# A four-layer decoder trunk on one core: the weights' parts begin at eight places, 4 bytes apart, and rotate through ten slots instead of eleven

## The chip, the cores and the metric

The kernel runs on one core of one Trainium2 chip. The metric is device time in microseconds (us) of one execution; the lower the better. The time before is 1584.25 us, the median of two runs (1583.47 and 1585.03 us).

Engines: PE (TensorE, matrix products), PEld (its loads of the stationary operand, which overlap the products), ACT (ScalarE), DVE (VectorE), POOL (GpSimd), SP (issues transfers).

## What is computed

Four residual layers over 256 tokens of width 1024, everything in float32. The token mixer is attention in layers 0 and 3, a gated short convolution in layer 1, a Conformer convolution in layer 2. A gated feed-forward block (FFN) of width 2816 follows in every layer.

```
def conv_ffn(x, w_in, w_conv, w_out):
    u = causal_dwconv(x @ w_in, w_conv)
    g, v = jnp.split(u, 2, axis=-1)
    return (jax.nn.silu(g) * v) @ w_out

    for i in range(DEPTH):
        a = rms_norm(h, mix_norm_pre[i])
        m = mixer of layer i (a)
        h = h + rms_norm(m, mix_norm_post[i])
        f = conv_ffn(rms_norm(h, ffn_norm_pre[i]), ffn_w_in[i], ffn_w_conv[i], ffn_w_out[i])
        h = h + rms_norm(f, ffn_norm_post[i])
```

## The kernel before, in words

**Products.** Activations lie transposed, 128 features on the partitions and 256 tokens along them. A float32 product is made of three products in the type float32r: every operand is split into a coarse part `hi` and a remainder `lo`, and `mm3` (L280 to L282) adds `hi`·x`hi`, `hi`·x`lo` and `lo`·x`hi` in PSUM. A weight block of 128 x 128 is the stationary operand and 256 columns of activations stream past it. `ramp` (L433, L438, L440) does the same in another order at a stage's start, and `Slabs.mm` (L522) for the FFN's second matrix. In attention's values (L878 to L880) the roles are exchanged: activations are stationary and 256 columns of weights stream. Each of these products loads its stationary operand anew.

**The stream of weights.** `Stream` hands the weights out in 480 pieces of 128 x 1024 float32, each used by 24 products. A piece is half of a 1 MB block `raw` (three buffers) that SP fetches from HBM. `first` (L186 to L194) lets ACT copy the piece to `whi` (L192, a cast), and `second` (L196 to L199) lets DVE form `wlo` = `raw` - `whi` (L198). Both parts go to rotating slots, `SLOTS` = 11 of each. `take` hands over the next piece and makes one on the spot if none is ready. `copy`, `diff` and `pump` are called between other work and make pieces in advance, as long as this holds:

```
if self.copied < min(len(self.pieces), self.used - self.held + self.slots - margin):
```

With `margin` = 1 at most 10 pieces are copied beyond those taken. No piece is made in `boundary`, the norm between two stages, except at the kernel's very start; what was made before must last until the next stage's calls of `between` (one `diff`, one `copy`).

**Order.** The whole program runs under a manual schedule: each engine executes its instructions in the order in which the code issues them. There is no planner.

**Addresses.** All tiles lie in fixed places. In the built program every `whi` and `wlo` slot begins 32 bytes past a multiple of 128 bytes on its partition, and every activation tile 96 bytes past one. A pad named `gap` (112 float32) at the head of the activations' pool fixes that distance of 64.

Of the kernel before, what the change touches and what calls it, by code (L numbers as in the profile page):

```python
# [11 lines left out]
F32R = mybir.dt.float32r  # L12
# [4 lines left out]
P = 128  # L17
# [3 lines left out]
KD = D // P  # L21
# [9 lines left out]
EPS_LN = 1e-5  # L31
BIG = 1e30
HKF = KF // 2
SLOTS = 11
NACT = 32
PE_TAPS = (13, 13, 13, 15)
SPLIT = 60
FIRST = 10
# [29 lines left out]
def plan():  # L68

    nt = 3 * NH * DH  # L70
    for l in range(DEPTH):
        kind, j = l % 3, l // 3
        if kind == 0:
            for quad in range(NQ):
                for what, g in order(quad):
                    if what == "v":
                        for k0 in (0, 4):
                            yield "attn_w_qkv", j, k0, 4, 2 * nt + (g * NH + 4 * quad) * DH, 2 * P
                    else:
                        c = (g * NH + 4 * quad + 2 * (what == "b")) * DH  # L80
                        yield "attn_w_qkv", j, 0, KD, c, P
                        yield "attn_w_qkv", j, 0, KD, nt + c, P
            for d in range(KD):
                yield "attn_w_o", j, 0, KD, d * P, P
        elif kind == 1:
            for step in sc_steps():
                if step[0] == "col":
                    for c in (D, 2 * D, 0):
                        yield "sc_w_in", j, 0, KD, c + step[1] * P, P
                elif step[0] == "slab":  # L90
                    yield "sc_w_out", j, step[1], 1, 0, D
                elif step[1] % 2 == 0:
                    yield "sc_w_out", j, SC_HEAD, KD - SC_HEAD, step[1] * P, 2 * P
        else:
            for k in range(KD):
                yield "cc_w_pw1", j, 0, KD, k * P, P
                yield "cc_w_pw1", j, 0, KD, D + k * P, P
            for d in range(KD):
                yield "cc_w_pw2", j, 0, KD, d * P, P
        for step in ffn_steps():  # L100
            if step[0] == "col":
                for c in (0, F):
                    yield "ffn_w_in", l, 0, KD, c + step[1] * P, P
            elif step[0] == "slab":
                yield "ffn_w_out", l, step[1], 1, 0, D
            else:
                yield "ffn_w_out", l, FF_HEAD, KF - FF_HEAD, step[1] * P, P
# [37 lines left out]
class Stream:  # L145
# [40 lines left out]
    def first(self):  # L186
        b, c, n = self.pieces[self.copied]
        self.load(b + self.ahead)
        hi = self.w_pool.tile([P, KD * P], F32R, tag="whi", name="whi")[:, :n * P]
        lo = self.w_pool.tile([P, KD * P], F32R, tag="wlo", name="wlo")[:, :n * P]  # L190
        raw = self.raw[b][:, c:c + n * P]
        self.nc.scalar.copy(out=hi, in_=raw)  # L192
        self.parts[self.copied] = hi, lo, raw
        self.copied += 1  # L194

    def second(self):  # L196
        hi, lo, raw = self.parts[self.prepped]
        self.nc.vector.tensor_tensor(out=lo, in0=raw, in1=hi.bitcast(F32), op=ALU.subtract)  # L198
        self.prepped += 1  # L199

    def copy(self, margin=1):
        if self.copied < min(len(self.pieces), self.used - self.held + self.slots - margin):
            self.first()
# [25 lines left out]
def trunk_kernel(ctx: ExitStack, tc: tile.TileContext, xT, pos, params, consts, masks, w8, out):  # L229
    nc = tc.nc  # L230
    cp = ctx.enter_context(tc.tile_pool(name="cp", bufs=1))
    rawp = ctx.enter_context(tc.tile_pool(name="rawp", bufs=3))
    wp = ctx.enter_context(tc.tile_pool(name="wp", bufs=SLOTS))
    ap = ctx.enter_context(tc.tile_pool(name="ap", bufs=1))
    ps = ctx.enter_context(tc.tile_pool(name="ps", bufs=1, space=bass.MemoryType.PSUM))
    ap.tile([P, 112], F32, tag="gap", name="gap")

    st = Stream(nc, rawp, wp, SLOTS, 3, [w8[i] for i in range(w8.shape[0])])
    for _, _, _, nk, _, cols in plan():
# [20 lines left out]

    def act(dt=F32, tag="act", bufs=NACT, shape=(P, 2, T)):
        counter[0] += 1
        return ap.tile(list(shape), dt, tag=tag, name=f"{tag}{counter[0]}", bufs=bufs)
# [15 lines left out]
    def mm3(o, whi, wlo, x, first, last):  # L279
        nc.tensor.matmul(o, lhsT=whi, rhs=x[0], start=first, stop=False)  # L280
        nc.tensor.matmul(o, lhsT=whi, rhs=x[1], start=False, stop=False)  # L281
        nc.tensor.matmul(o, lhsT=wlo, rhs=x[0], start=False, stop=last)  # L282
# [142 lines left out]
    def ramp(xs, os, hook=None):  # L425


        ws = [st.take() for _ in os]
        alone = [i == 0 or os[i - 1].tensor is not o.tensor for i, o in enumerate(os)]

        def second(k):
            for o, (whi, wlo, _) in zip(os, ws):
                nc.tensor.matmul(o, lhsT=whi[:, k, :], rhs=xs[k][1], start=False, stop=k == KD - 1,  # L433
                                 skip_group_check=True)

        for k in range(KD):
            for o, (whi, wlo, _), a in zip(os, ws, alone):
                nc.tensor.matmul(o, lhsT=whi[:, k, :], rhs=xs[k][0], start=k == 0 and a, stop=False,  # L438
                                 skip_group_check=True)
                nc.tensor.matmul(o, lhsT=wlo[:, k, :], rhs=xs[k][0], start=False, stop=False,  # L440
                                 skip_group_check=True)
            if k:
                second(k - 1)
        if hook:
            hook()
        second(KD - 1)
        return os
# [212 lines left out]
    def conformer(l, mg, rb):  # L660
# [7 lines left out]
        def cols(q, hook=None):  # L668
            if q > 1:
                banks[q % 2] = [psum("A") for _ in range(2)]  # L670
            for bank in banks[q % 2]:
                for o in halves(bank):
                    column(xs, o, hook)
                    hook = None
# [50 lines left out]

        mine = [list(range(CONV - 1 - n, CONV - 1)) for n in PE_TAPS]
        rest = [list(range(CONV - 1 - n)) for n in PE_TAPS]
        cols(1, scale)
# [65 lines left out]
    def attention(l, mg, rb):  # L794
# [125 lines left out]
        def weigh(pair, pts):  # L920
            o = psum("B")
            quad, q2 = divmod(pair, 2)

            def mm(hp, g, kc, cols, blk, first, last):
                col = (2 * q2 + hp) * DH
                nc.tensor.matmul(o[hp * DH:(hp + 1) * DH, cols], lhsT=vs[quad, g][:, kc, col:col + DH],  # L926
                                 rhs=pts[hp][blk // 2][:, blk % 2, cols], start=first, stop=last)

            for kc in range(2):
                for hp in range(2):  # L930
                    mm(hp, 0, kc, slice(0, T), kc, kc == 0, False)
            for g in (1, 2):
                for c in range(2):
                    for hp in range(2):
                        mm(hp, g, c, slice(c * P, (c + 1) * P), 1 + g, False, g == 2 and c == 1)
            ys[pair] = two()
            split(ys[pair], o[:, :T])
# [264 lines left out]
```

## Time and profile before

| | before |
|---|---|
| median of two runs | 1584.25 us |
| the profiled execution: its own time | 1583.57 us |
| the profiled execution: span, first to last instruction | 1581.7 us |
| PE busy | 1555.7 us (98%) |
| DVE busy | 1243.0 us (79%) |
| ACT busy | 925.2 us (58%) |
| read from HBM | 253.87 MB |

The span is what the rows below add up to; some 1.9 us of the execution lie around it. Products overlap in the profile: one lasts some 280 ns, but the next begins after 113 to 118 ns, so the pace is read from starts, not from durations. In the rows, `psA` and `psB` are PSUM tiles, `act` and `tmp` are activations, `raw`, `whi` and `wlo` are the stream's tiles.

### The profile page before, as it was taken

The page shows a single profiled execution, that of the slowest core. Times are in us where ns is not written, and L with a number is a line of the kernel's source. Part 1 is how long each engine was busy: PE and PEld are TensorE (multiplying, and loading weights), DVE is VectorE, ACT ScalarE, POOL GpSimd, SP SyncE. Part 2 cuts the span into 40 slices and gives each one's busy share as a digit, 9 for nine tenths or more (in the row PEclk, how much of TensorE's full clock was granted, in tenths as well). Part 3 has the DMA queues.
Part 4 walks back from the last instruction along what each step waited for, and adds up shares of the span by engine and source line. Part 5 has one row for each costly group of instructions (what it writes and reads, how often), then busy time and mean ns, then how long its engine had stood idle before and what let it go on. Part 6 is the DMA issues. An engine that isn't in the chain of part 4 may idle for free.

```text
span 1581.7 us, 31426 instructions
## 1 busy us (share of the span) xinstructions
PE 1555.7 (98%) x13146; PEld 1520.5 (96%) x13146; DVE 1243.0 (79%) x2177; ACT 925.2 (58%) x1623; POOL 17.9 (1%) x51
## 2 busy tenths in 40 slices
PE   6999999999999999999999999999999999999998
PEld 6999999999999999999999999999999999999997
DVE  4997877697876779889599598786887778588783
ACT  6564655575564566656477666565655445566562
POOL 4000000000000000000000000000000000000000
PEclk9999999999999999999999999999999999999999
DMA  5653543265552644655243136554453434236540
GB/s 218 216 212 131 176 145 108 99 232 204 187 190 100 217 161 162 238 187 184 110 144 124 54 118 239 197 174 153 178 192 138 161 134 160 107 134 237 190 160 28
DMA packets 36718, 256.94 MB, mean 162 GB/s; under 512 B 4320, under 2 KB 4448, under 8 KB 5984
## 3 DMA queue, kind: packets, MB, share of 16 engines
q1 hardware_dynamic: 36288, 254.93, 45.0%
q8 instruction: 103, 1.69, 0.4%
q14 instruction: 39, 0.32, 0.1%
q10 hardware_dynamic: 288, 0.01, 0.0%
HBM read 253.87 MB, written 1.05 MB: 161 GB/s over the span
## 4 chain that ended last, share of the span: by engine, by line
PE 93%; DVE 3%; ACT 1%; POOL 1%; issue 1%; DMA 1%; DVEq 0%; ACTq 0%; POOLq 0%
PE psA L522 17%; PE psB L282 10%; PE psB L280 10%; PE psB L281 10%; PE psA L280 7%; PE psA L281 7%; PE psA L282 7%; PE psA L878 3%; PE psA L880 3%; PE psA L879 3%; PE psB L715 2%; PE psB L926 2%; PE psB L897 2%; PE psA L438 2%; PE psB L915 2%; PE psA L433 2%
## 5 line engine op out<-in xcount | busy, mean ns | idle before, releaser
L198 DVE TENSOR_TENSOR wlo<-raw,whi 128x1024 fp32r<-128x1024 f32 x480 | 580.7, 1221 | 35.3 <-ACT whi L192 34.4
L192 ACT CAST whi<-raw 128x1024 fp32r<-128x1024 f32 x480 | 490.9, 1048 | 23.8 <-DMA raw<-in_w_dram 18.7
L282 PE MATMUL psB<-act,wlo 128*128 128x256 f32 x1392 | 390.7, 281 | 0.0
L280 PE MATMUL psB<-act,whi 128*128 128x256 f32 x1392 | 390.7, 281 | 0.0
L281 PE MATMUL psB<-act,whi 128*128 128x256 f32 x1392 | 390.7, 281 | 0.0
L280 PE MATMUL psA<-act,whi 128*128 128x256 f32 x1040 | 299.2, 288 | 8.0 <-ACT whi L192 7.1
L282 PE MATMUL psA<-act,wlo 128*128 128x256 f32 x1040 | 290.7, 280 | 0.5 <-DVE wlo L198 0.5
L281 PE MATMUL psA<-act,whi 128*128 128x256 f32 x1040 | 290.8, 280 | 0.2
L522 PE MATMUL psA<-act,whi 128*128 128x256 f32 x1536 | 272.9, 281 | 0.0
L281 PEld LDWEIGHTS psB<-act,whi 128*128 128x128 f32 x1392 | 265.0, 190 | 0.0
L282 PEld LDWEIGHTS psB<-act,wlo 128*128 128x128 f32 x1392 | 263.1, 189 | 0.0
L280 PEld LDWEIGHTS psB<-act,whi 128*128 128x128 f32 x1392 | 261.3, 188 | 0.0
L522 PEld LDWEIGHTS psA<-act,whi 128*128 128x128 f32 x1536 | 236.2, 189 | 0.0
L522 PE MATMUL psA<-act,wlo 128*128 128x256 f32 x768 | 215.8, 281 | 0.0
L280 PEld LDWEIGHTS psA<-act,whi 128*128 128x128 f32 x1040 | 196.9, 189 | 12.8 <-ACT whi L192 7.1
L282 PEld LDWEIGHTS psA<-act,wlo 128*128 128x128 f32 x1040 | 197.1, 190 | 0.8 <-DVE wlo L198 0.8
L281 PEld LDWEIGHTS psA<-act,whi 128*128 128x128 f32 x1040 | 197.2, 190 | 0.6 <-DVE act L285 0.5
L291 ACT ACTIVATE tmp<-act,par 128x256 f32<-128x256 f32 x176 | 80.2, 503 | 167.5 <-DVE act L285 167.5
L288 DVE SCALAR_TENSOR_TENSOR tmp<-act,par,tmp 128x255 f32<-128x255 f32 (+1 forms) x352 | 146.7, 480 | 19.7 <-ACT tmp L291 19.7
L522 PEld LDWEIGHTS psA<-act,wlo 128*128 128x128 f32 x768 | 145.2, 189 | 0.0
L285 DVE TENSOR_TENSOR act<-psB,act 128x512 f32<-128x512 f32 (+2 forms) x94 | 58.5, 626 | 89.1 <-PE psB L282 52.2
L878 PE MATMUL psA<-whi,act 128*128 128x256 f32 x384 | 111.0, 289 | 0.0
(124 smaller groups left out, 2116.1 us busy)
## 6 DMA issues: line engine op xcount, KB each, us to landing
raw<-in_w_dram SPq DMA_DIRECT2D x239, 1024.0 KB, 4.8
h<-in_xT_dram SPq DMA_DIRECT2D x4, 256.0 KB, 5.0
raw<-in_w_dram SPq DMA_DIRECT2D x2, 512.0 KB, 5.5
out_dram<-h SPq DMA_DIRECT2D x4, 256.0 KB, 2.0
msk<-in_masks_dram SPq DMA_DIRECT2D x1, 512.0 KB, 9.3
par<-in_params_dram SPq DMA_DIRECT2D x1, 484.0 KB, 10.0
cst<-in_consts_dram SPq DMA_DIRECT2D x1, 132.0 KB, 5.9
par<-in_params_dram ACTq DMA_DIRECT2D x1, 4.0 KB, 2.9
```

What stands on the lines that cost most here:

```text
L192: self.nc.scalar.copy(out=hi, in_=raw)
L198: self.nc.vector.tensor_tensor(out=lo, in0=raw, in1=hi.bitcast(F32), op=ALU.subtract)
L280: nc.tensor.matmul(o, lhsT=whi, rhs=x[0], start=first, stop=False)
L281: nc.tensor.matmul(o, lhsT=whi, rhs=x[1], start=False, stop=False)
L282: nc.tensor.matmul(o, lhsT=wlo, rhs=x[0], start=False, stop=last)
L285: nc.vector.tensor_tensor(out=out, in0=a, in1=b, op=op)
L288: nc.vector.scalar_tensor_tensor(out=out, in0=a, scalar=s, in1=b, op0=op0, op1=op1)
L291: nc.scalar.activation(out=out, in_=a, func=AF.Identity, scale=s, bias=b)
L522: nc.tensor.matmul(o, lhsT=a, rhs=b, start=first and i == 0, stop=last and i == 2, skip_group_check=True)
L878: nc.tensor.matmul(oc, lhsT=xh, rhs=whi[:, k % 4, :], start=k == 0, stop=False)
L879: nc.tensor.matmul(oc, lhsT=xh, rhs=wlo[:, k % 4, :], start=False, stop=False)
L880: nc.tensor.matmul(oc, lhsT=xl, rhs=whi[:, k % 4, :], start=False, stop=k == KD - 1)
```

## The change

Three things change.

1. Each part gets a tile 64 elements (`ROOM`) longer than a piece, and begins inside it at an offset of 28 to 35 elements: 28 + (i // 3) % 8 for piece i. Three pieces in a row begin at each place, then the next three 4 bytes further on, and after eight places it starts over. `whi` and `wlo` of one piece begin at the same offset.
2. The longer tile is 4352 bytes instead of 4096, again a multiple of 128, so in the built program the parts begin 16, 20, 24, 28, 32, 36, 40 and 44 bytes past a multiple of 128. The fifth place is the one of before. The activations stay at 96.
3. `SLOTS` is 10, so at most 9 pieces are copied beyond those taken.

```
-SLOTS = 11
+SLOTS = 10
 NACT = 32
+ROOM = 64
...
     def first(self):
         b, c, n = self.pieces[self.copied]
         self.load(b + self.ahead)
-        hi = self.w_pool.tile([P, KD * P], F32R, tag="whi", name="whi")[:, :n * P]
-        lo = self.w_pool.tile([P, KD * P], F32R, tag="wlo", name="wlo")[:, :n * P]
+        at = self.shift(self.copied)
+        hi = self.w_pool.tile([P, KD * P + ROOM], F32R, tag="whi", name="whi")[:, at:at + n * P]
+        lo = self.w_pool.tile([P, KD * P + ROOM], F32R, tag="wlo", name="wlo")[:, at:at + n * P]
         raw = self.raw[b][:, c:c + n * P]
...
+    def shift(self, i):
+
+        return 28 + i // 3 % 8
```

PE, SP and POOL execute the same instructions in the same order as before. On DVE and ACT the smaller number of slots moves one piece in two places, and each move is undone later. On DVE the first lies in the first attention layer, between two heads' softmax steps (the two ISA rows and the reciprocal are the row minimum and the normalisation of one block of scores). Before:

```order
L904 ISA act_1200,tiny_1201<-psB_1188,msk 128x512
L904 ISA tiny_1201 128x1
L198 TENSOR_TENSOR wlo<-raw,whi 128x1024
L908 RECIPROCAL tiny_1203<-tiny_1202 128x1
L909 TENSOR_SCALAR act_1200<-act_1200,tiny_1203 128x512
L904 ISA act_1214,tiny_1215<-psB_1189,msk 128x512
```

With the change (line numbers are 6 higher there):

```order
L910 ISA act_1200,tiny_1201<-psB_1188,msk 128x512
L910 ISA tiny_1201 128x1
L914 RECIPROCAL tiny_1203<-tiny_1202 128x1
L915 TENSOR_SCALAR act_1200<-act_1200,tiny_1203 128x512
L910 ISA act_1208,tiny_1209<-psB_1189,msk 128x512
```

A subtraction for the stream is gone from here. From this place on the n-th subtraction stands where the (n+1)-th stood, so every piece is made one turn later relative to the products that use it, until the conformer of layer 2 begins, where the stream catches up. It falls behind again inside the conformer and catches up for good at the end of the last FFN, where the second row of order on DVE is (`act_19073` and `act_19081` are the last gated activations' remainders). Before:

```order
L198 TENSOR_TENSOR wlo<-raw,whi 128x1024
L285 TENSOR_TENSOR act_19073<-tmp_18987,act_19073 128x256
L285 TENSOR_TENSOR tmp_19061<-tmp_19060,tmp_19061 128x256
L198 TENSOR_TENSOR wlo<-raw,whi 128x1024
L285 TENSOR_TENSOR act_19081<-tmp_19061,act_19081 128x256
L198 TENSOR_TENSOR wlo<-raw,whi 128x1024 x2
L288 SCALAR_TENSOR_TENSOR tmp_19242<-tmp_19242,tmp_19215 128x256
```

With the change:

```order
L200 TENSOR_TENSOR wlo<-raw,whi 128x1024
L291 TENSOR_TENSOR act_19069<-tmp_18983,act_19069 128x256
L291 TENSOR_TENSOR tmp_19057<-tmp_19056,tmp_19057 128x256
L200 TENSOR_TENSOR wlo<-raw,whi 128x1024
L291 TENSOR_TENSOR act_19077<-tmp_19057,act_19077 128x256
L200 TENSOR_TENSOR wlo<-raw,whi 128x1024 x3
L294 SCALAR_TENSOR_TENSOR tmp_19242<-tmp_19242,tmp_19215 128x256
```

Three subtractions close the last FFN's first part where two did. ACT's casts move in the same way.

## Rows read from the trace of the kernel before

**Rows 1.** The profile's page: span, busy time of the engines, and the clock granted to PE in 40 slices.

```profile
span 1581.7 us, 31426 instructions
...
PE 1555.7 (98%) x13146; PEld 1520.5 (96%) x13146; DVE 1243.0 (79%) x2177; ACT 925.2 (58%) x1623; POOL 17.9 (1%) x51
...
PEclk9999999999999999999999999999999999999999
```

**Rows 2.** All instructions by line and form: times they occur, busy time, mean ns of one, and idle time of the engine before them. First PE's products with weights (480 pieces x 24), then the two steps that make a piece.

```profile
L282 PE MATMUL psB<-act,wlo 128*128 128x256 f32 x1392 | 390.7, 281 | 0.0
L280 PE MATMUL psB<-act,whi 128*128 128x256 f32 x1392 | 390.7, 281 | 0.0
L281 PE MATMUL psB<-act,whi 128*128 128x256 f32 x1392 | 390.7, 281 | 0.0
...
L522 PE MATMUL psA<-act,whi 128*128 128x256 f32 x1536 | 272.9, 281 | 0.0
L522 PE MATMUL psA<-act,wlo 128*128 128x256 f32 x768 | 215.8, 281 | 0.0
...
L198 DVE TENSOR_TENSOR wlo<-raw,whi 128x1024 fp32r<-128x1024 f32 x480 | 580.7, 1221 | 35.3 <-ACT whi L192 34.4
...
L192 ACT CAST whi<-raw 128x1024 fp32r<-128x1024 f32 x480 | 490.9, 1048 | 23.8 <-DMA raw<-in_w_dram 18.7 <-PE psA L281 4.9
```

**Rows 3.** PE in order of time, two stretches without a break; start (us) and duration (us) of single products. The L280 rows begin one group of three each. First the FFN of layer 1, the first and the last of 14 such rows.

```profile
604.17 0.28 PE L280 MATMUL psA<-act,whi 128*128 128x256 f32 x1
...
608.76 0.28 PE L280 MATMUL psA<-act,whi 128*128 128x256 f32 x1
...
1122.20 0.28 PE L280 MATMUL psA<-act,whi 128*128 128x256 f32 x1
...
1126.96 0.28 PE L280 MATMUL psA<-act,whi 128*128 128x256 f32 x1
```

The last two are from attention in layer 3, the first and the last of 15.

**Rows 4.** PE's products by line and form in four stretches of the first attention layer that follow each other without a break: 41 to 46 us, 47 to 51.5, 52 to 57 and 58 to 63. Mean ns of one stands after the busy time. L878 to L880 have activations stationary, L280 to L282 weights.

```profile
L879 PE MATMUL psA<-wlo,act 128*128 128x256 f32 x15 | 4.2, 279 | 0.0
...
L281 PE MATMUL psA<-act,whi 128*128 128x256 f32 x14 | 3.9, 276 | 0.0
...
L879 PE MATMUL psA<-wlo,act 128*128 128x256 f32 x15 | 4.1, 276 | 0.0
...
L281 PE MATMUL psA<-act,whi 128*128 128x256 f32 x15 | 4.2, 281 | 0.0
```

**Rows 5.** Busy time of PE in five stretches of 20 us, with the products in them, the granted clock, DMA share and GB/s: conformer output and following, then the FFN of layers 0, 1, 2 and 3.

```profile
884.00:904.00 20.00, 20.00 (x178) 1.00 0.16 54
344.00:364.00 20.00, 20.00 (x172) 1.00 0.70 259
650.00:670.00 20.00, 20.00 (x172) 1.00 0.60 222
1010.00:1030.00 20.00, 20.00 (x172) 1.00 0.54 197
1500.00:1520.00 20.00, 20.00 (x172) 1.00 0.53 197
```

**Rows 6.** What PE waited for: us in total, times, longest.

```profile
PE psA L280 <- ACT whi L192: 7.1, 1, 7.1
...
PE psA L282 <- DVE wlo L198: 0.5, 1, 0.5
```

**Rows 7.** Merged PE rows in the conformer: L715 streams 256 columns whose start moves by 4 bytes from one tap to the next (52 passes, each tap 4); L724 streams from one fixed alignment (16 passes). Start, duration of the whole; behind them the same two groups by line and form, with the mean ns of one pass.

```profile
801.14 11.39 PE L715 MATMUL psB<-act,tmp 128*128 128x256 f32 x52
...
870.39 3.62 PE L724 MATMUL psS<-act,cst 128*128 128x256 f32 x16
...
L715 PE MATMUL psB<-act,tmp 128*128 128x256 f32 x156 | 34.2, 378 | 0.0
...
L724 PE MATMUL psS<-act,cst 128*128 128x256 f32 x16 | 3.6, 379 | 0.0
```

**Rows 8.** DVE's multiply-and-add of the conformer's taps by form, start shifted 4 bytes per tap (242 elements: 14 places, 226 elements: 30 places).

```profile
L288 DVE SCALAR_TENSOR_TENSOR act<-act,par,act 128x237 f32<-128x237 f32 x8 | 3.4, 476 | 0.0
...
L288 DVE SCALAR_TENSOR_TENSOR act<-act,par,act 128x236 f32<-128x236 f32 x8 | 3.4, 472 | 0.0
L288 DVE SCALAR_TENSOR_TENSOR act<-act,par,act 128x235 f32<-128x235 f32 x8 | 3.4, 469 | 0.0
L288 DVE SCALAR_TENSOR_TENSOR act<-act,par,act 128x234 f32<-128x234 f32 x8 | 3.4, 468 | 0.0
```

**Rows 9.** DVE at the start of layer 1's FFN: the stream's subtractions (start, duration).

```profile
600.08 1.22 DVE L198 TENSOR_TENSOR wlo<-raw,whi 128x1024 fp32r<-128x1024 f32 x1
...
603.39 1.22 DVE L198 TENSOR_TENSOR wlo<-raw,whi 128x1024 fp32r<-128x1024 f32 x1
...
606.43 1.23 DVE L198 TENSOR_TENSOR wlo<-raw,whi 128x1024 fp32r<-128x1024 f32 x1
```

**Rows 10.** PE at the same place: the first product with `wlo` of four columns that follow each other (one column is one piece, 24 products).

```profile
600.87 0.28 PE L282 MATMUL psA<-act,wlo 128*128 128x256 f32 x1
...
603.70 0.28 PE L282 MATMUL psA<-act,wlo 128*128 128x256 f32 x1
...
606.53 0.28 PE L282 MATMUL psA<-act,wlo 128*128 128x256 f32 x1
...
609.35 0.28 PE L282 MATMUL psB<-act,wlo 128*128 128x256 f32 x1
```

**Rows 11.** The start of layer 3's attention: DVE's subtractions (the second row is five in a row), and the first product with `wlo` of the column that needs the first of them.

```profile
1120.87 1.22 DVE L198 TENSOR_TENSOR wlo<-raw,whi 128x1024 fp32r<-128x1024 f32 x1
...
1125.16 5.76 DVE L198 TENSOR_TENSOR wlo<-raw,whi 128x1024 fp32r<-128x1024 f32 x5
...
1124.81 0.28 PE L282 MATMUL psA<-act,wlo 128*128 128x256 f32 x1
```

## The prediction

> **What bounds the kernel now.** I read the page first: PE is busy for 1555.7 of 1581.7 us, at full clock nearly throughout, while DVE idles a fifth of the span and ACT two fifths [rows 1]. Then PE's waits: it waited for a piece of weights 7.1 us at the very start and 0.5 us once later [rows 6]. So nothing feeds PE late, and the time is the number of products times their pace. The products with weights are 480 x 24 = 11,520; five of their groups stand in [rows 2].
>
> The view that decides is then the order of time on PE. In the FFN, 13 groups of three take 608.76 - 604.17 = 4.59 us, or 117.7 ns from start to start. In layer 3's attention the same three lines, with the same shapes, take (1126.96 - 1122.20) / 42 = 113.3 ns [rows 3]. So the kernel runs at one of two paces, **slow** and **quick**, 4.4 ns apart. The granted clock is 1.00 in both [rows 5], so this isn't the clock. The duration marks the pace: 281 ns in a slow stretch, 276 in a quick one. All four FFN stretches count 172 products in 20 us, the quick stretch 178 [rows 5], and the groups that only FFN and column work fill have a mean of 281 [rows 2]: 3 x 1392 + 1536 + 768 = 6,480 products are slow. For the other 5,040 (attention, `ramp`, conformer columns) both paces occur, and I take half as quick, an estimate: 9,000 slow, 2,520 quick.
>
> What sets the pace? Four stretches that follow each other without a break [rows 4]: activations stationary, slow (279); weights stationary, quick (276); activations again, still quick (276); weights again, slow (281). Thus the same lines with the same addresses run at either pace, a pace holds while nothing changes, and going over to stationary weights (the load's start moves from 96 to 32 bytes past 128, the stream's from 32 to 96) turned it, once each way. I read this as two paces that lock in, with a change of the operands' relative start as what can turn one into the other.
>
> **The change part by part.**
>
> *Eight places.* Instruction counts and sizes are unchanged; only the start addresses of `whi` and `wlo` move. On PE the relative start now jumps by 4 bytes after every third piece, 160 jumps in all, and by 28 bytes back after eight of them. A jump itself costs at most what such a turn costs, a few ns; 160 of them are under 1 us. What counts is the pace behind it. No row has a load of weights that starts elsewhere than 32 or 96, so I bound it. From below: if every slow product became quick, 9,000 x 4.4 ns = 40 us are saved. From above: if every quick one became slow, 2,520 x 4.4 = 11 us are lost; and if an odd start made each load dearer in itself, more (rival 2). If jumps turn the pace, now this way, now that way, half of the 11,520 are quick behind them: 5,760 - 2,520 = 3,240 more than now, a gain of 14.3 us. I take this value: turns happen in this trace at changes of the relative start [rows 4], and the FFN, where nothing moves for hundreds of products, holds the stock of slow ones.
>
> Does a start off its place cost something by itself? The nearest row is the conformer's tap product: its stream starts 4 bytes further for each tap, and 52 passes take 11.39 us, (11.39 - 0.38) / 51 = 215.9 ns each. The mean product, always at one alignment, takes (3.62 - 0.38) / 15 = 216.0 [rows 7]. So for the streamed operand an odd start is free. That is no proof for the stationary one, whose load is what two following products leave no slack for. The Trainium skill (SBUF — State Buffer, on SBUF "cachelines") says that SBUF is read in lines of 16 bytes and that crossing into a new line costs; by it a load of 128 float32 touches 33 lines instead of 32 at six of the eight places, an estimate from that section of 117.7 / 32 = 3.7 ns x 8,640 products = 32 us. By that rule the sum would be 32 us higher; the trace's one row on odd starts shows no such cost, so the sum goes by the row.
>
> On ACT and DVE the parts are written (and `whi` read back) at the same odd places. DVE's taps start 4 bytes further each time and shrink steadily with their size, 476, 472, 469, 468 ns, with no saw-tooth [rows 8]: free. For ACT no row writes at odd places; a cast is 1048 ns per piece [rows 2], and PE needs 24 x 117.7 ns = 2.82 us for one, so even a quarter more (262 ns x 480 = 126 us) fits into ACT's 656 idle us. Taken as nothing.
>
> *Ten slots.* One piece fewer is ready when a stage's norm starts, and after it each piece's subtraction comes one turn later. Where the lead is over 2.83 us it is hidden: in the FFN's course the lead is some 18 us and PE waits nowhere [rows 6]. It is thin at three starts. In layer 1's FFN the subtractions end at 601.30, 604.61 and 607.66 [rows 9], for columns whose first `wlo` product stands at 603.70, 606.53 and 609.35 [rows 10]: leads of 2.40, 1.92 and 1.69. Moved one turn, they serve the columns of 600.87, 603.70 and 606.53, and are late by 0.43, 0.91 and 1.13 us; a wait moves the products behind it, so the largest counts: 1.13 us. Layer 2's FFN runs the same code, 1.13 again. At layer 3's attention the subtraction that ends at 1122.09 serves 1124.81; its successor, which takes its place, ends at 1126.38 [rows 11]: 1.57 late. Sum 3.8 us. Bounds: nothing, if DVE is ahead there, and one whole piece at each, 3 x 2.82 = 8.5 us. Queued behind the waiting product are all later ones; DVE's evacuations wait for them, but DVE then only idles.
>
> **Sum.** Profiled execution 1583.57 us: -14.3 + 3.8 = -10.5 gives 1573; the median of runs lies 0.7 us above that execution, so 1574.
>
> **Rivals.**
>
> 1. *Nothing turns.* A jump of 4 bytes is small beside the 64 of the roles' exchange, and going from weights to activations didn't turn the pace in [rows 4]. Then only the slots cost: 1584.25 + 3.8 = 1588.
> 2. *Odd loads cost (the other side).* For it: loads bound the pace, and a quicker and a slower load is what the two paces look like. If the step between the paces, 4.4 ns, is paid once more by each product at the seven places other than the present one, 10,080 x 4.4 = 44 us: 1584 + 4 + 44 = 1632. Against it: [rows 7]. It is slower by over 2% from (31.7 - 3.8) / 10,080 = 2.8 ns per such product on. The Trainium skill's line rule, above, would give 1584 + 4 + 32 = 1620.
> 3. *All becomes quick.* Quick holds across a change of roles in [rows 4], so a jump may end a slow stretch and never start one: -40 + 4, 1548.
>
> **How the numbers follow.** Chances: jumps turn both ways 0.42 (1574, by itself 1562 to 1585), nothing turns 0.23 (1588), odd loads cost 0.22 (1595 to 1632), all quick 0.13 (1545 to 1562). A measurement of this kernel tells about 2%, 31.7 us, from no change: faster is below 1552.6, slower above 1615.9. Two thirds of rival 3 lie below the one, 0.09; two thirds of rival 2 above the other, 0.15; 0.76 between. The range leaves out about the same: 1553 to 1620.
>
> **What would show it.** In the profile after, the FFN should fall into stretches of three pieces (72 products, some 8.3 us) at 276 and 281 ns, changing at the jumps; L522 and L280 of `psB` should have means of 278 or 279. Means of 281 throughout speak for rival 1, durations beyond 281 at most of the places for rival 2, 276 throughout for rival 3. PE's waits should show `wlo` with 1 to 2 us at the three starts, at most one piece each; if they come to over 9 us, the slots were undervalued. L198 and L192 should keep 1221 and 1048 ns within a few per cent. The prediction is wrong if a single place sets a pace of its own that neither 276 nor 281 describes, or if a stage's start turns PE's clock down, which no row of [rows 1] suggests.

## The result and the profile after

The changed kernel takes 1604.72 us (median of 2 runs, 1604.15 to 1605.3): 1.0134 times the kernel before, interval 1.0116 to 1.0153. So it is 1.3% slower, 20.5 us, where 10 us less were forecast. The profiled execution has a span of 1602.2 us.

The page after, its figures for PE and the groups that answer to [rows 1, 2]; a group's last figures are busy time, mean ns of one, and idle time before it.

```profile
span 1602.2 us, 31432 instructions
...
PE 1574.5 (98%) x13146; PEld 1537.3 (96%) x13146; DVE 1243.5 (78%) x2177; ACT 924.8 (58%) x1623; POOL 17.5 (1%) x51
...
PEclk9999999999999999999999999999999999999999
...
L200 DVE TENSOR_TENSOR wlo<-raw,whi 128x1024 fp32r<-128x1024 f32 x480 | 580.2, 1220 | 43.5 <-ACT whi L194 41.9
L194 ACT CAST whi<-raw 128x1024 fp32r<-128x1024 f32 x480 | 490.5, 1047 | 22.2 <-DMA raw<-in_w_dram 17.9
L288 PE MATMUL psB<-act,wlo 128*128 128x256 f32 x1392 | 391.3, 281 | 0.0
L286 PE MATMUL psB<-act,whi 128*128 128x256 f32 x1392 | 390.7, 281 | 0.0
L287 PE MATMUL psB<-act,whi 128*128 128x256 f32 x1392 | 390.3, 280 | 0.0
```

PE's busy time rose by 18.8 us against [rows 1], at the same instructions and the same clock. ACT's cast and DVE's subtraction, now at odd places, kept 1047 and 1220 ns [rows 2]. The groups that the FFNs fill most, forecast at 278 or 279, stayed at 280 and 281. The mean hides what happens below it. Busy time of PE in five stretches of 8.4 us in layer 0's FFN, each inside three pieces at one place; the places are `at` = 32, 34, 35, 28 and 29, or 32, 40, 44, 16 and 20 bytes past a multiple of 128. (x..) counts the products, those cut by an edge too.

```profile
382.30:390.70 8.40, 8.40 (x74) 1.00 0.66 225
...
399.30:407.70 8.40, 8.40 (x73) 1.00 0.62 225
407.80:416.20 8.40, 8.40 (x70) 1.00 0.39 145
416.60:425.00 8.40, 8.40 (x74) 1.00 0.62 217
425.10:433.50 8.40, 8.40 (x74) 1.00 0.40 153
```

And PE's groups in the third of these stretches, by line and form.

```profile
L287 PE MATMUL psB<-act,whi 128*128 128x256 f32 x23 | 6.6, 286 | 0.0
L288 PE MATMUL psB<-act,wlo 128*128 128x256 f32 x22 | 6.3, 287 | 0.0
L286 PE MATMUL psB<-act,whi 128*128 128x256 f32 x22 | 6.3, 286 | 0.0
```

There are stretches of three pieces, as forecast, but none of these is quick. At seven places the products keep the slow pace or a little more (by their starts 117.5 to 118.3 ns), at the eighth, 44 bytes, they are slower than anything before: 286 ns, 123 from start to start. Behind an FFN's first pieces a place gives the same pace at each of its turns, except in the first round of layer 1: there 44 bytes ran at 120.0 ns, and 20 bytes at 113.5, the only quick visit in the four FFNs.

Attention lost more. PE in three stretches of 40 us of layer 0's attention, first the kernel before.

```profile
60.00:100.00 40.00, 39.77 (x362) 1.00 0.58 212
100.00:140.00 40.00, 40.00 (x366) 1.00 0.46 158
140.00:180.00 40.00, 40.00 (x369) 1.00 0.45 159
```

The same stretches after the change.

```profile
60.00:100.00 40.00, 40.00 (x359) 1.00 0.59 211
100.00:140.00 40.00, 40.00 (x360) 1.00 0.38 132
140.00:180.00 40.00, 40.00 (x361) 1.00 0.48 168
```

What PE waited for after the change, the row of [rows 6] that moved:

```profile
PE psA L288 <- DVE wlo L200: 2.8, 6, 1.3
```

Adding up PE's start-to-start times by stage in both traces, after minus before, in us; the second row counts the pieces alone whose subtraction ends late:

| | att. 0 | FFN 0 | short conv. | FFN 1 | conformer | FFN 2 | att. 3 | FFN 3 | sum |
|---|---|---|---|---|---|---|---|---|---|
| all | 4.4 | 1.5 | 0.4 | 2.1 | 1.1 | 2.7 | 7.0 | 1.5 | 20.7 |
| of it late pieces | | | | 1.3 | | 1.3 | 1.7 | | 4.2 |

So some 16 us are pace, three fifths of it in the two attention layers, and 4.2 us stand at just the three starts that the prediction named.

### The profile page after: what moved, and what is told of

Its sections match the earlier page's. It is cut to its first block, busy times and chain, and to the rows that moved or that the text cites. A ratio compares the mean times of both kernels' runs of the same rounds, so it can differ in the third digit from the quotient of the medians.

```text
span 1602.2 us, 31432 instructions
## 1 busy us (share of the span) xinstructions
PE 1574.5 (98%) x13146; PEld 1537.3 (96%) x13146; DVE 1243.5 (78%) x2177; ACT 924.8 (58%) x1623; POOL 17.5 (1%) x51
## 4 chain that ended last, share of the span: by engine, by line
PE 90%; DVE 6%; ACT 1%; POOL 1%; issue 1%; DMA 1%; DVEq 0%; ACTq 0%; POOLq 0%
PE psA L528 17%; PE psB L288 10%; PE psB L287 10%; PE psB L286 10%; PE psA L286 7%; PE psA L288 6%; PE psA L287 6%; PE psA L884 3%; PE psA L885 3%; PE psA L886 3%; DVE act L294 2%; PE psB L903 2%; PE psB L932 2%; DVE wlo L200 2%; PE psA L444 2%; PE psB L921 2%
## 5 line engine op out<-in xcount | busy, mean ns | idle before, releaser
L200 DVE TENSOR_TENSOR wlo<-raw,whi 128x1024 fp32r<-128x1024 f32 x480 | 580.2, 1220 | 43.5 <-ACT whi L194 41.9
L194 ACT CAST whi<-raw 128x1024 fp32r<-128x1024 f32 x480 | 490.5, 1047 | 22.2 <-DMA raw<-in_w_dram 17.9
L286 PE MATMUL psB<-act,whi 128*128 128x256 f32 x1392 | 390.7, 281 | 0.0
L286 PE MATMUL psA<-act,whi 128*128 128x256 f32 x1040 | 301.2, 290 | 7.8 <-ACT whi L194 6.9
L286 PEld LDWEIGHTS psB<-act,whi 128*128 128x128 f32 x1392 | 262.0, 188 | 0.0
L286 PEld LDWEIGHTS psA<-act,whi 128*128 128x128 f32 x1040 | 196.8, 189 | 12.7 <-ACT whi L194 6.9
```

## The experiments

One thing about addresses is needed for all of them. A part's tile was 4096 bytes long and is 1088 x 4 = 4352 = 17 x 256, so all tiles still begin alike: 32 bytes past a multiple of 256. Activations begin 224 past one. `at` = 32, the "present" place modulo 128, is thus 160 modulo 256. The **distance** (activations minus weights, modulo 256) was 192 in the kernel before; in the change it is 80 to 52, and 192 doesn't occur. Unless a diff is against the kernel before, it is against the changed kernel, and all kernels with `shift` have ten slots except the last.

**Slots alone, and one place alone.**

```diff
-        return 28 + i // 3 % 8
+        return 32
```

> Ten slots with the longer tiles, but all parts at the present place (32 bytes past 128). Places theory (the 20 us come from where the parts begin): only the three late starts cost, 1586 to 1588 us. Slots theory (the shorter lead costs more than the waits show): 1600 us or more.

Measured: 1595.42 us, 1.0102 [1.0072, 1.0132], between the two times expected. This is far more than the slots' 4 us, with nothing turning; the place modulo 128 isn't all.

```diff
-        return 28 + i // 3 % 8
+        return 35
```

> All parts at 44 bytes past 128, no jumps. Places theory (a place has a pace of its own): the FFN runs at 123 ns where it ran at 117.8, 6336 products x 5.1 ns = 32 us, attention at 119 to 120 instead of some 115.5, 12 us more: 1625 to 1640 us. Jumps theory (it is the changes every third piece that throw the pace off): nothing jumps, 1584 to 1592 us.

Measured: 1610.06 us, 1.0221 [1.0169, 1.0272], again between the two. PE in 20 us of the FFN of layers 0 to 3:

```profile
430.00:450.00 20.00, 20.00 (x179) 1.00 0.48 162
720.00:740.00 20.00, 20.00 (x164) 1.00 0.51 180
1010.00:1030.00 20.00, 20.00 (x179) 1.00 0.61 210
1500.00:1520.00 20.00, 20.00 (x164) 1.00 0.52 196
```

One address, two outcomes: 113.3 ns in two layers, 123.3 in the other two, each held from the ninth piece at the latest to the FFN's end. Ahead of that the pace changes where something interrupts the row of weight products: in layer 1 they ran at 120.0, at 113.3 behind small products of the norm, at 120.0 behind PE's first two waits for late pieces, and at 123.3 behind the third. So a place offers a set of paces, another set than the present place's, and an interruption at a stage's start can pick another of them.

**A map of 32 places, and the same with the activations moved.** Each FFN holds a place for eight pieces and goes up by 4 bytes; elsewhere `at` = 0. The second kernel moves the activations by 32 bytes.

```diff
-        return 28 + i // 3 % 8
+        return next((8 * k + (i - b) // 8 for k, b in enumerate((80, 178, 268, 414)) if b <= i < b + 64), 0)
```

> In each FFN the place moves on by 4 bytes after eight pieces: 32 places over the four FFNs cover all of 128 bytes; elsewhere the present place. Places theory: one steady pace in each stretch of eight pieces, with the places of the changed kernel as there (16 to 40 bytes 117.5 to 118.3 ns, 44 bytes 123), and 1590 to 1615 us. Jumps theory: no pace but 113.3 and 117.8, whatever the place.

```diff
...
-    ap.tile([P, 112], F32, tag="gap", name="gap")
+    ap.tile([P, 120], F32, tag="gap", name="gap")
```

> As map_up, with the activations 32 bytes further on (a pad of 120 instead of 112 elements). If the distance between stationary and streamed operand sets the pace, the whole pattern moves by 32 bytes (123 ns at 76 bytes instead of 44). If the place of the load alone sets it, the pattern stays (123 ns at 44).

Measured, one execution each: 1592.46 and 1602.68 us. PE in the first map with weights at 44, 48, 52 and 56 bytes past 256 (layer 0), 20 us in each:

```profile
366.50:386.50 20.00, 20.00 (x178) 1.00 0.61 211
388.30:408.30 20.00, 20.00 (x171) 1.00 0.56 206
411.10:431.10 20.00, 20.00 (x169) 1.00 0.55 193
434.20:454.20 20.00, 20.00 (x179) 1.00 0.52 185
```

In the second at 76, 80, 84 and 88 (layer 1):

```profile
660.80:680.80 20.00, 20.00 (x179) 1.00 0.59 211
682.60:702.60 20.00, 20.00 (x171) 1.00 0.56 205
705.40:725.40 20.00, 20.00 (x169) 1.00 0.55 193
728.40:748.40 20.00, 20.00 (x179) 1.00 0.54 186
```

The row of paces moved along with the activations, by the same 32 bytes, down to the tenth of a ns: by starts 113.4, 118.8, 119.9 and 113.5 in both, means over the eight pieces. The two maps have 24 distances in common. Three of them lie at the start of an FFN; of the other 21, 19 agree within 0.1 ns and two don't (148: 120.0 and 122.2; 140: 118.3 and 119.0). So the pace belongs to the distance, not to the weights' address, and most distances give 117.7 ns or more. Distance 180 (and 168) is quick in both. The 123 ns expected at 44 bytes in the first map didn't come, because 44 past 256 is another place than the change's, 172.

**128 bytes.** The old distance with ten slots; the change with activations 128 bytes further, which makes its distances 208 to 180; and the kernel before with the activations alone moved so (distance 64, that of the slots-only kernel).

```diff
-        return 28 + i // 3 % 8
+        return 0
```

> As slots_only, but the parts begin at the head of the longer tile, 128 bytes earlier: 32 past a multiple of 256, where the kernel before has them and slots_only has 160. Distance theory in 256 bytes (the pace hangs on the distance of weights and activations taken modulo 256, so slots_only had moved): attention back at 115.2 to 115.5 ns from 116.5, and only the late starts cost, 1584 to 1590 us, 5 to 10 below slots_only. If 128 bytes are the unit: the same as slots_only, 1594 to 1596.

```diff
-    ap.tile([P, 112], F32, tag="gap", name="gap")
+    ap.tile([P, 144], F32, tag="gap", name="gap")
```

> The changed kernel with the activations 128 bytes further on, so that its fifth place has the distance of the kernel before modulo 256 too. Distance theory in 256 bytes: at least the pieces of the fifth place in attention are quick, and the other places show another set of paces than in the changed kernel; 1590 to 1605 us. If 128 bytes are the unit: the changed kernel again, 1604 us with the same paces at the same places (44 bytes 123 ns in the FFN).

The same edit in the kernel before:

> The kernel before, eleven slots and nothing shifted, with only the pad of the activations 128 bytes longer: the distance of slots_only without its late starts. Distance theory in 256 bytes: attention at 116.5 ns, no quick FFN, 1588 to 1592 us, some 3 to 6 below slots_only. If 128 bytes made no difference and slots_only's loss were the slot: 1578 to 1585, as before.

Measured: 1575.59 us, 0.995 [0.9934, 0.9966]; 1591.0 us, 1.0055 [1.0037, 1.0074]; 1588.4 us, 1.0025 [1.0016, 1.0035]. The first differs from the slots-only kernel by 128 bytes alone and is 20 us shorter (0.995 against 1.0102 by ratio). That 256 bytes are enough as a unit is seen in each kernel that holds a place: its slots lie 17 x 256 bytes apart, and the pace doesn't change from one slot to the next. PE in the first kernel's FFNs of layers 1 and 2:

```profile
700.00:720.00 20.00, 20.00 (x179) 1.00 0.50 179
1010.00:1030.00 20.00, 20.00 (x179) 1.00 0.49 165
```

And in the slots-only kernel's:

```profile
700.00:720.00 20.00, 20.00 (x172) 1.00 0.47 172
1010.00:1030.00 20.00, 20.00 (x172) 1.00 0.52 191
```

Distance 192 can run at either pace in an FFN, here quick in two of four where [rows 5] were slow in all, and that is why this kernel beats the one before in spite of its ten slots. The two are the FFNs whose start waits for late pieces. PE in layer 1's start of this kernel: the L286 group ahead of the first wait, two products in a row around the wait, and the L286 group behind it.

```profile
L286 PE MATMUL psA<-act,whi 128*128 128x256 f32 x3 | 0.8, 281 | 0.0
...
600.64 0.28 PE L287 MATMUL psA<-act,whi 128*128 128x256 f32 x1
601.23 0.38 PE L288 MATMUL psA<-act,wlo 128*128 128x256 f32 x1 [0.31 <-DVE wlo L200]
...
L286 PE MATMUL psA<-act,whi 128*128 128x256 f32 x7 | 1.9, 276 | 0.0
```

The pace turned from 117.7 to 113.3 ns at the wait. It did so at the waits of layer 2's FFN too, and in the same two FFNs of the kernel with a few steps, below, which starts them at distance 192. In layers 0 and 3 of both, and in all four FFNs of the kernel before, no such wait stands, and distance 192 ran slow behind the first pieces. So the waits that ten slots bring seem to have turned the pace. That they are the cause is argued, not shown: no run has such a wait without the smaller number of slots, and single executions of the kernel before went down to 1574.34 us, with no trace that says why.

At distance 64 all four FFNs were slow in both kernels that have it, and the loss by 128 bytes in the kernel before, 4 us by the medians and 8 between the two profiled executions, is attention's and the conformer's, whose mean paces by starts went from 115.4 to 116.5 and from 115.7 to 117.7 ns. Their distance being the same, these two kernels differ in the slots and the tiles' length. Between their traces it is 1.3, 1.3 and 1.5 us at the three late starts, 0.4 in the conformer and 4.3 in all (spans 1593.9 and 1589.6), though 7.0 between the medians, which come from two chips. So of the slots-only kernel's loss some 4 us are the slots', as forecast, and the rest is the distance.

The changed kernel's own loss shrinks by 13.7 us when only its activations are moved by these 128 bytes. Its rotation in layer 1's FFN, at weights 20, 24, 28 and 32 bytes past 128, 8 us each:

```profile
637.50:645.50 8.00, 8.00 (x73) 1.00 0.73 287
645.70:653.70 8.00, 8.00 (x70) 1.00 0.82 297
654.20:662.20 8.00, 8.00 (x69) 1.00 0.48 146
662.80:670.80 8.00, 8.00 (x73) 1.00 0.50 178
```

There the present distance (192, the last row) is among the eight, and is quick; with 20 and 44 bytes (204, 180) three of the eight are, the others between 117.7 and 119.7.

**The rotation in the FFNs alone,** `at` = 0 elsewhere.

```diff
-        return 28 + i // 3 % 8
+        return 28 + i // 3 % 8 if any(b <= i < b + 66 for b in (80, 178, 268, 414)) else 0
```

> The changed kernel, but its places only for the FFNs' pieces; attention, short convolution and conformer keep the distance of the kernel before modulo 256. Distance theory: what attention and conformer lost comes back, 9 to 13 us: 1590 to 1596 us. If what attention lost hangs on the slots or on the jumps in the FFN: 1600 to 1605.

Measured: 1595.72 us, 1.0072 [1.0057, 1.0087]: 9.0 us below the change, and 1.2% above the kernel with `at` = 0 throughout, by their ratios (0.995). The rotation thus costs some 9 us outside the FFNs, about what the table has for attention, and in the FFNs what it costs hangs on the pace that they would have had otherwise.

**Holding a distance.**

```diff
-        return 28 + i // 3 % 8
+        return 6
```

> All parts 24 bytes past the place of before (56 past a multiple of 256), the other place of the map at 113.5 ns. If a place that ran quick on the map does so in every FFN: 1558 to 1568 us. If held_at3's steady quick pace is a thing of that place alone and here both paces occur: 1570 to 1600.

```diff
-        return 28 + i // 3 % 8
+        return 3
```

> All parts 12 bytes past the place of before (44 past a multiple of 256; held_44 was at 172). Distance theory in 256 bytes: the stretch of the map at this place ran at 113.35 ns, so the FFN may run at that throughout, 6312 products x 4.4 ns = 28 us less, attention unknown: 1555 to 1590 us. Theory that the pace is drawn anew at each stage's start: FFNs at 113 or 123 as in held_44, 1590 to 1615 us.

Measured: `at` = 6 (distance 168) 1589.89 us, 1.0038 [1.0021, 1.0056], with single runs from 1582.45 to 1594.49; `at` = 3 (distance 180) 1560.11 us, 0.9857 [0.9838, 0.9877]. At 168, quick in the map, the FFNs counted 169, 174, 179 and 169 products in 20 us: this distance has several paces too. At 180, PE in the FFNs of layers 0 to 3:

```profile
430.00:450.00 20.00, 20.00 (x179) 1.00 0.47 159
700.00:720.00 20.00, 20.00 (x179) 1.00 0.54 183
1010.00:1030.00 20.00, 20.00 (x179) 1.00 0.51 184
1480.00:1500.00 20.00, 20.00 (x179) 1.00 0.45 159
```

All four quick, against 172 throughout in [rows 5]. Attention isn't: its mean is 115.3 ns, as before.

**A few steps to the good distance.** `at` = 0 except in each FFN, where 36, 40 and then 44 bytes follow after 8, 10 and 12 pieces and the last stays.

```diff
-        return 28 + i // 3 % 8
+        return next((max(0, min(3, (i - b - 6) // 2)) for b in (80, 178, 268, 414) if b <= i < b + 66), 0)
```

> The present place everywhere, but in each FFN the place moves by 4 bytes after 8, 10 and 12 pieces, as it did in the map ahead of its stretch at 113.35 ns, and then stays. If the way to a place decides which of its paces is taken: 4 x 53 x 24 products x 4.4 ns = 22 us less than slots_at0, 1562 to 1570 us. If the start of a stage decides: no more than half of that, 1575 to 1590 us.

Measured: 1566.45 us, 0.9899 [0.9879, 0.9919]. In layer 1 the pieces ran at 118.3 ns at 36 and 40 bytes and at 113.3 from the first piece at 44 on; all four FFNs went quick there. A step of 4 bytes does turn the pace, onto what the distance offers.

**The good distance with eleven slots,** `wlo` keeping ten, and the pad cut so that the distance stays 180.

```diff
-SLOTS = 10
+SLOTS = 11
...
-        lo = self.w_pool.tile([P, KD * P + ROOM], F32R, tag="wlo", name="wlo")[:, at:at + n * P]
+        lo = self.w_pool.tile([P, KD * P + ROOM], F32R, tag="wlo", name="wlo", bufs=SLOTS - 1)[:, at:at + n * P]
...
-        return 28 + i // 3 % 8
+        return 3
...
-    ap.tile([P, 112], F32, tag="gap", name="gap")
+    ap.tile([P, 48], F32, tag="gap", name="gap")
```

> held_at3 with eleven slots for the coarse parts and ten for the remainders, the pad shortened by 256 bytes to make room, so that the distance stays modulo 256. If the late starts come from the smaller number of pieces made ahead: they go, 3 to 6 us less than held_at3, 1554 to 1557. If the remainders' ten slots make them: 1560 as held_at3.

Measured: 1554.27 us, 0.9809 [0.9794, 0.9823], 5.8 us below ten slots, and 30 below the kernel before. PE's wait for `wlo`, and one in the conformer, with ten slots:

```profile
PE psA L288 <- DVE wlo L200: 3.7, 7, 1.3
PE psB L721 <- ACT tmp L297: 1.5, 2, 1.3
```

With eleven the second is gone, and of the first is left:

```profile
PE psA L288 <- DVE wlo L200: 0.5, 1, 0.5
```

The same three products in order of time with ten slots, in the FFNs of layers 0, 2 and 3:

```profile
351.27 0.28 PE L528 MATMUL psA<-act,whi 128*128 128x256 f32 x1
...
950.38 0.28 PE L528 MATMUL psA<-act,whi 128*128 128x256 f32 x1
...
1419.13 0.28 PE L528 MATMUL psA<-act,whi 128*128 128x256 f32 x1
```

With eleven:

```profile
351.31 0.28 PE L528 MATMUL psA<-act,whi 128*128 128x256 f32 x1
...
946.01 0.28 PE L528 MATMUL psA<-act,whi 128*128 128x256 f32 x1
...
1412.96 0.28 PE L528 MATMUL psA<-act,whi 128*128 128x256 f32 x1
```

The two are level before the first thin start, 4.4 us apart behind the second, and 6.2 behind the third and at the end (spans 1558.4 and 1552.2). By stages the slot is paid at the three starts (1.6, 1.6 and 1.8 us) and in the conformer (1.2), where products of the taps wait for ACT with ten slots. The rows of waits show less than the delays, since a wait is counted from the end of the product before, and products overlap: at the wait shown above, 0.31 us stand in the row, but the start came 0.59 us after the last instead of 0.12.

## Why the prediction was wrong, point by point

**What bounds the kernel** was read rightly: PE at the pace of its weight products, two of which stood in [rows 3], and the pace alone makes 50 us between kernels with ten slots (1560 and 1610). The estimate of 2,520 quick products was close: of 11,383 start-to-start times between two weight products in the trace before, 2,509 are under 115.5 ns. Half of the 5,040 had been assumed, so this is luck.

**The step that failed** is "half of the 11,520 are quick behind them", the term of -14.3 us; in its place stood about +16. Two things were wrong in it. First, the prediction took the relative start modulo 128 and so the fifth place for the present one. The map and the 128-byte kernels show that the distance counts modulo 256: the change left the present distance altogether. Second, it took two paces that a jump throws at random. The runs show a set of paces for each distance, of which a jump or a start picks one. The eight distances of the change offered 117.5 ns and more, but for rare visits, one of them (52) a pace of 123.3 ns that the kernel before never showed; and in `held_44`, where the same distance was held, 113 ns was open to it as well. The sentence "wrong if a single place sets a pace of its own that neither 276 nor 281 describes" named what came. [Rows 4] were read too boldly. When the roles change, the distance changes its sign too (192 becomes 64), so these rows hold two distances, and at 192 the same lines ran at 276 the first time and at 281 the second. They show that a pace can be picked anew when something changes; they don't show that a jump of 4 bytes turns slow into quick as often as quick into slow.

The bound of 11 us, for every quick product becoming slow, is nearest to what happened; it was passed by 5 us because paces beyond 117.7 were priced under rival 2 alone.

**The slots** were right in mechanism and place, and nearly in size: 3.8 forecast, 4.2 in the change (1.3, 1.3 and 1.7 where 1.13, 1.13 and 1.57 stood). At the quick distance the slot costs more, 5.0 us at the three starts and 1.2 in the conformer, a place that the sum didn't have; the medians make it 5.8, inside the bound of 8.5. What the sum left out is that a late start can change the pace behind it.

**Odd starts** cost nothing, as the sum assumed. ACT's and DVE's rows kept their durations, and the fastest kernels of all load weights at 44 bytes, 12 past a multiple of 32, at 276 ns. The line rule of the Trainium skill (SBUF — State Buffer, on SBUF "cachelines") would have made such a load dearer than one at 32; this case's runs don't show that. Rival 2 as a mechanism falls with it: in the FFNs only one of the eight places was dearer by more than 0.6 ns than the slow pace of before. That the measured time lies in rival 2's band (1595 to 1632), and so in the range of 1553 to 1620, is luck. Rival 1's time (1588) lay nearer than the forecast, but not its reason: the pace did change. Rival 3 falls for this choice of places; at distance 180 it is nearly what happens in the FFNs. The two shares of two thirds that gave 0.09 and 0.15 don't come out of the bands: spread evenly over them, it would be 0.45 and 0.43, and 0.85 in place of 0.76 between.

Not settled: why a distance has the paces that it has, what decides which one an interruption picks, and why attention takes little part in the gain at 180.

## What to carry to other kernels

Where a stream of weight loads and products bounds a kernel, compare start-to-start times of the same line in several stages: levels some per cent apart at full clock can be the distance between the two operands' addresses, and padding one tile moves it. Map distances by holding each for some pieces within one kernel, over all of 256 bytes (the two maps here cover 160), and hold the good one in a run of its own, since 168 was quick on the map and not in every FFN; a rotation over unknown ones averages over paces of which most are poor. A kernel whose pace can be picked anew at each stage's start needs several runs, and a version that fixes the pace is worth more than its mean.

## What the runs showed of the hardware that wasn't expected

- The pace of 128x128 loads with 256-column products, at a granted clock of 1.00, took values of 113.3, 116.7, 117.8, 118.3, 119.2, 120.0, 122.2 and 123.3 ns, steady within a stretch; which of them are open is set by the operands' distance modulo 256 bytes (19 of 21 distances at the same pace in two kernels whose activations lie 32 bytes apart).
- Where a distance has more than one, an FFN keeps the one that it has behind its first eight pieces to its end, 58 pieces or more (held at 44 bytes past 128: x179 and x164 in 20 us, layer by layer).
- At distance 192 the pace turned from 117.7 to 113.3 ns at a wait of PE, in four FFN starts of four in two kernels.
- The quickest stretches seen, 113.3 ns, have the shortest durations shown too (276 ns); 286 goes with 123.3.
